# Loading and turning the second half's input in counted steps of the v block and the next, a longer end of the mLSTM, and written order up to the last projection block

## The chip, the core and the metric

The kernel runs on one core of a Trainium2 chip. The metric is device time in microseconds (us) for one execution. PE is the matrix engine; its weight loads have a row of their own, PEld. DVE is the vector engine, ACT the scalar engine and POOL the GpSimd engine. SP issues the DMAs. Each engine carries out its own instructions strictly in the order in which the program lists them, and waits on semaphores for the others.

## What is computed

One layer of a hybrid decoder trunk on 2048 positions of 1024 channels, in fp32. Cut to what matters here:

```python
h = rms_norm(x, g_mix) * (1 + sc1) + sh1
p = h @ w_in            # q_a k_a v_a | q_m k_m v_m o_m | u_s v_s | gates
y_attn  = forgetting_attention(rms(q_a), rms(k_a), v_a, f_a)   # 8 heads of 64
y_mlstm = sigmoid(o_m) * rms(mlstm_chunkwise(q_m, k_m, v_m, i_m, f_m))
y_sgu   = spatial_gating(gelu(u_s), gelu(v_s))
x = x + gt1 * (concat(y_attn, y_mlstm, y_sgu) @ w_out)
x = x + gt2 * conv_ffn(rms_norm(x, g_ffn) * (1 + sc2) + sh2)
```

The change touches the first part alone: the norm of x, the projections p, and the mLSTM that runs beside them.

## The kernel before

**Products.** Every fp32 operand is split into a high and a low part, and a product is three matmuls (`mm3`, lines 54 to 56: high by high, high by low, low by high). The sequence is cut into two halves of 1024 positions, and each half into 8 row tiles of 128. `hT[tb, k]` holds h turned (channels on the partitions) for one block `tb` of 512 positions and one of 8 channel groups `k`, as a high tile `hh` and a low tile `hl`.

**Blocks.** The projection runs as 14 steps, n = 0 to 13: seven blocks of columns of `w_in` for the first half (n = 0 to 6), then the same seven for the second (n = 7 to 13). The order of the seven is km with the gates (272 columns), qm and om (512), vm (256), the spatial gating's u and v (512), attention k (512), attention q (512), attention v (512). A block has eight row tiles; one row tile is 8 x 3 matmuls into a PSUM tile `acc`. There are three such tiles until the last block and two in it (`n_accs`). After a row tile a consumer reads it. In the v block this is `use_v` (line 754): twice per row tile, ACT casts 256 columns to the high part (line 761), DVE subtracts for the low part (line 762), and SP stores the pair to `v_d` (line 763). The pair is a tile `vhl` of the tag `q2k`, which has three buffers, shared with `qn` of the q block.

**Ticks.** `tick` (line 627) is the hook through which other work is laid between the matmuls. It runs at the end of each row tile and, in a block of 512 columns, also in its middle (after k = 3), so a wide block has 16 ticks and a narrow one 8. A tick runs what is due (`after(n, f)` puts a function n ticks ahead, such as the turning of q), one step of `rest_of_mod` in a middle tick (one DMA of a 256 KB piece `wa` of `w_ada`, one DVE operation on the piece before), and one step of the first generator in the list `background`: `rows`, `mlstm`, and in the last block `scores`. A generator gives the turn back at each `yield`. `products` (line 599) also loads (`load`) and casts (`cast`) the weights of the next block: one load at the end of each of the row tiles 0 to 6 and one in tile 7, the casts from tile 4 on, four of them in tile 7 and the last behind the block.

**The mLSTM's end.** `mlstm(qi)` handles 512 positions in 21 ticks. In its last five (lines 1027 to 1055) DVE divides H, ACT squares it into `hq` (line 1038), DVE reduces (line 1040), POOL raises to the power -0.5 (line 1042), two ticks on DVE multiplies into `hq` (line 1045), and two further ticks on PE turns `hq` (line 1052).

**The second half's input.** At step 6 four tiles of x are asked for (`load_x`, line 402). At step 7, ahead of the km block's matmuls, `make_h(2, x0)` and `make_h(3)` (line 555) norm and turn the half's two blocks: per row tile two squares on ACT (line 518), the mean and power, a multiplication on DVE (line 523); per channel group four transposes on PE (line 560), an ACT activation (line 564) and a DVE cast and subtraction (lines 565, 566).

**Who sets the order.** Steps 1 to 5 and 8 to 12 stand in a `manual_schedule`: there the order on each engine is that of the program's text. Steps 0, 6, 7 and 13 are ordered by a scheduler, which may draw an instruction forward past others, also into a written stretch. Step 13 closes the pools of the projection's side, opens attention's, loads k, the forget bias `nf`, q and the first half of v of head 0 (`load_k`, `load_q`, `load_v`), and puts the scores of head 0's first two blocks into `background`, from its first tick on.

Of the kernel before, what the change touches and what calls it, by code (L numbers as in the profile page):

```python
# [17 lines left out]
P = 128  # L18
S = 2048
D = 1024  # L20
DFF = 2816
NH = 8
EPS = 1e-6
NEG = -1.0e30
TB = 512
KT = D // P
# [7 lines left out]
def trunk(  # L34
# [43 lines left out]
    ident = cst.tile([P, P], F32, name="ident")  # L78
# [11 lines left out]
    a1 = cst.tile([P, KT], F32, name="a1")  # L90
    sh1 = cst.tile([P, KT], F32, name="sh1")
# [280 lines left out]
    def tr_ps():  # L372
        return pp.tile([P, 512], F32, name="trp", tag="trp")

    def misc_ps():
        return pp.tile([P, 512], F32, name="mp", tag="mp")
# [25 lines left out]
    def load_x(tt):  # L402
        xt = pool.tile([P, D], F32, name="xt", tag="t4k")
        dma(xt, x[tt * P : (tt + 1) * P, :])
        return xt
# [17 lines left out]
    def rest_of_columns():  # L423
        r = pool.tile([P, P], F32, name="rows", tag="tmpA")
        dma(r[0:8], g_ffn[0].rearrange("(k p) -> k p", p=P))
        for i, g in enumerate((g_q, g_k)):
            for j in range(2):
                dma(r[8 + i : 9 + i, 64 * j : 64 * j + 64], g)
        dma(r[10:14], b_s[0])
        dma(r[14:16], g_m_out[0].rearrange("(k p) -> k p", p=P))  # L430
        transposed(colA[:, 24:40], r, 16)
        V.tensor_scalar(gq8, colA[:, 32:33], 0.125, None, op0=ALU.mult)
# [80 lines left out]
    def norm_x(xin):  # L513
        for xt in xin:
            st = pool.tile([P, 2], F32, name="st", tag="st")
            for q in range(2):
                jk = pool.tile([P, 512], F32, name="jk", tag="sq")
                A.activation(jk, xt[:, q * 512 : q * 512 + 512], AF.Square, accum_out=st[:, q : q + 1])
            V.tensor_tensor(st[:, 0:1], st[:, 0:1], st[:, 1:2], op=ALU.add)
            st = st[:, 0:1]  # L520
            V.tensor_scalar(st, st, 1.0 / D, EPS, op0=ALU.mult, op1=ALU.add)
            rsqrt(st, 1)
            V.tensor_scalar(xt, xt, st, None, op0=ALU.mult)
        return xin

    x0 = norm_x([load_x(i) for i in range(4)])
# [7 lines left out]
    def head_setup():  # L534
        rest_of_columns()
        dma(gsgu, g_sgu.broadcast_to([P, 256]))
        dma(gbias[:, 0:8], b_fox_f.broadcast_to([P, 8]))
        dma(gbias[:, 8:12], b_m_i.broadcast_to([P, 4]))
        dma(gbias[:, 12:16], b_m_f.broadcast_to([P, 4]))
        wsn = pool.tile([P, 4, P], F32, name="wsn", tag="sq")  # L540
        dma(wsn, w_s[0].rearrange("g t s -> t g s"))
        for g in range(4):
            G.affine_select(
                wsn[:, g, :], wsn[:, g, :], pattern=[[-1, P]], compare_op=ALU.is_ge, fill=0.0,
                base=0, channel_multiplier=1,
            )
        ps = misc_ps()
        for g in range(4):
            T.transpose(ps[:, g * P : (g + 1) * P], wsn[:, g, :], ident)
        A.copy(wT.rearrange("p g t -> p (g t)"), ps)  # L550


    hT = {}

    def make_h(tb, xin=None):
        xs = xin if tb == 0 else norm_x(xin or [load_x(tb * 4 + i) for i in range(4)])
        for k in range(KT):
            ps = (tr_ps, acc_ps)[k % 2]() if tb == 0 else tr_ps()
            for i in range(4):
                T.transpose(ps[:, i * P : (i + 1) * P], xs[i][:, k * P : (k + 1) * P], ident)  # L560
            h32 = pool.tile([P, TB], F32, name="h32", tag="t2k")
            hh = pool.tile([P, TB], F32R, name="hh", tag="hT")
            hl = pool.tile([P, TB], F32R, name="hl", tag="hT")
            A.activation(h32, ps, AF.Identity, bias=sh1[:, k : k + 1], scale=a1[:, k : k + 1])
            V.tensor_copy(hh, h32)
            V.tensor_tensor(hl, h32, hh.bitcast(F32), op=ALU.subtract)  # L566
            hT[tb, k] = (hh, hl)


    class Weights:  # L570
# [51 lines left out]
    pending = []  # L622
    chores, started = [], []
    background = []
    ticks = [0]

    def tick(middle=False):
        ticks[0] += 1
        due()
        if middle and chores and started and next(chores[0], True):  # L630
            chores.pop(0)
        if background and next(background[0], True):
            background.pop(0)
# [19 lines left out]
    def due(everything=False):  # L653
        for item in pending[:]:
            if everything or item[0] <= ticks[0]:
                pending.remove(item)
                item[1]()
# [267 lines left out]
    def mlstm(qi):  # L925
        t0 = qi * 512
        neb = nebs[qi % 2]
        ecol, acol, dcol = cols[qi]
        H = pool.tile([P, 4, 4, 65], F32, name="H", tag="H")
# [48 lines left out]
        for n in range(4):  # L978
            kT, M1 = got["k", n], got["M", n]
            kn, qT, v1 = got["l", n]  # L980
            qz = qzs[n % 2]
            sc = pool.tile([P, 4, P], F32, name="sc", tag="sc")
# [53 lines left out]
        dma(om, om_d[:, :, t0 : t0 + 512].rearrange("j p t -> p j t"))  # L1036
        hq = pool.tile([P, 4, 4, 64], F32, name="hq", tag="t4k")
        A.activation(hq, hn, AF.Square)
        ss = pool.tile([P, 4, 4], F32, name="mss", tag="mss")
        V.tensor_reduce(ss, hq, axis=AX.X, op=ALU.add)  # L1040
        V.tensor_scalar(ss, ss, 1.0 / 64, EPS, op0=ALU.mult, op1=ALU.add)
        G.tensor_tensor(ss, ss, nhalf[:, 0:1].unsqueeze(2).broadcast_to([P, 4, 4]), op=ALU.pow)
        yield
        yield
        V.tensor_tensor(hq, hn, bc(ss, 3, 64), op=ALU.mult)
# [21 lines left out]
    nb = len(blocks)  # L1067
    steps = [(h, i) for h in range(2) for i in range(nb)]
    chores.append(rest_of_mod())
    written = ExitStack()  # L1070
# [4 lines left out]
        cur.cast()  # L1075
    first_mod(1)
    for n, (half, i) in enumerate(steps):
        if i == 0:
            make_h(half * 2, x0)
            if half == 0:  # L1080
                head_setup()
            make_h(half * 2 + 1)
        elif n == nb - 1:
            x0 = [load_x(8 + t) for t in range(4)]
        if n == len(steps) - 1:
            while background:
                if next(background[0], True):
                    background.pop(0)
            n_accs[0] = 2
            pool.close("proj_r")  # L1090
            pp.close("proj_r")
            attention_open_right()

            load_k(0)
            first_rows = [], []
            first = [scores(0, tb, load_q(0, tb, "qA"), r) for tb, r in zip((1, 0), first_rows)]
            load_v(0, (0, 1))
            background += first
        nxt[0] = Weights(blocks[steps[n + 1][1]][0]) if n + 1 < len(steps) else None
        if i == 1:  # L1100
            written.enter_context(tc.manual_schedule())
        blocks[i][1](half, cur)
        started.append(n)
        if nxt[0]:
            nxt[0].cast()
        cur = nxt[0]
        if n in (nb - 2, 2 * nb - 2):
            written.close()
        if i == 0:
            log_gates(half)  # L1110
            background += [rows(half * 2), rows(half * 2 + 1)]
        if i == 2:
            background.append(mlstm(half * 2 + 1))
        if n == nb + 2:
            small_setup()
    while pending:
        due(True)
    pool.close("proj_l")
    pp.close("proj_l")

# [37 lines left out]
    hT = {}  # L1158
# [33 lines left out]
    class Block:  # L1192
# [466 lines left out]
    for i, s in enumerate(steps):  # L1659
# [33 lines left out]
        if i:  # L1693
            q = steps[i - 1]
# [51 lines left out]
```

## Time and profile before

| | us |
|---|---|
| median of 3 runs | 2610.47 |
| lowest and highest | 2605.68, 2610.91 |
| the profiled execution | 2607.8 |
| its span on the core | 2606.1 |

The profiled execution lies 2.7 below the median of the three. The span is the stretch from the first instruction to the last, and 1.7 lies around it. The page of the profile gives each engine's busy time; a PE that is busy isn't a PE at its peak, because overlapping matmuls are counted as busy at any pitch. The view of waits lists, for one engine, the idle time before its instructions and what ended it. The timeline lists instructions in order of time: start, duration, engine, line, operation, what is written and read, and in square brackets the idle time of the engine before it. The view of windows gives busy time for each engine in a stretch, the granted PE clock (PEclk), and the DMA engines' share and rate. The projection fills the first 711 us of the span; the rest is attention, the output projection and the channel MLP.

### The profile page before, as it was taken

To read this page: it belongs to the slowest core of one execution; us is meant where nothing else is said; L and a number is where in the kernel's file an instruction comes from. 1 tells how busy PE (TensorE), PEld (TensorE's weight loads), DVE (VectorE), ACT (ScalarE), POOL (GpSimd) and SP (SyncE) were. 2 spreads that over 40 slices of the span, in tenths; PEclk is the share of its full clock that TensorE was granted. 3 is DMA by queue.
4 is the path that set the end of the run, shared out by engine and by line. 5 is a ranking of instruction groups with operands and counts; after the bars stand their busy time and mean duration, and the time that the engine had idled before them with its cause. 6 is when DMAs were issued, how large, how long until landed. Compare 5 with 4: busy or idle time off the path is not lost.

```text
span 2606.1 us, 36311 instructions
## 1 busy us (share of the span) xinstructions
PE 2530.5 (97%) x12521; PEld 2097.9 (81%) x12537; DVE 2010.0 (77%) x3438; ACT 1272.8 (49%) x2424; POOL 402.5 (15%) x532
## 2 busy tenths in 40 slices
PE   5999999999999999999989999999999999999999
PEld 5888888888787877777868888888888888888787
DVE  7657666476388889866589888888888887997797
ACT  4333343432388878844455544454444444444443
POOL 2012310132266556520000000000000000000000
PEclk9999999999999999999999999999999999999999
DMA  7345763454664445266632222255222217658523
GB/s 247 107 120 160 209 209 88 129 152 138 180 164 123 129 126 166 58 195 224 248 89 92 79 89 82 81 201 187 90 81 81 90 65 279 210 176 290 184 93 117
DMA packets 302592, 379.58 MB, mean 146 GB/s; under 512 B 31934, under 2 KB 194588, under 8 KB 300360
## 3 DMA queue, kind: packets, MB, share of 16 engines
q1 hardware_dynamic: 302408, 377.26, 46.1%
q8 instruction: 99, 1.62, 0.3%
q14 instruction: 85, 0.70, 0.1%
HBM read 276.44 MB, written 100.74 MB: 145 GB/s over the span
## 4 chain that ended last, share of the span: by engine, by line
PE 81%; DVE 9%; DMA 4%; ACT 3%; issue 2%; POOL 1%; SPq 0%; DVEq 0%; ACTq 0%; POOLq 0%
PE ub L56 11%; PE ub L54 11%; PE ub L55 11%; PE acc L54 6%; PE acc L56 6%; PE acc L55 6%; PE db L55 4%; PE db L56 4%; PE db L54 4%; PE sp L206 3%; PE tp L259 3%; PE op L245 2%; PE op L246 2%; PE wps L55 2%; PE wps L54 2%
## 5 line engine op out<-in xcount | busy, mean ns | idle before, releaser
L54 PE MATMUL acc<-wh,hh 128*128 128x512 f32 (+2 forms) x768 | 285.5, 373 | 1.9 <-DVE vhl L762 1.2
L54 PE MATMUL ub<-T,wsph 128*128 128x512 f32 x704 | 274.2, 390 | 5.8 <-ACT wsph L1358 5.8
L56 PE MATMUL ub<-T,wspl 128*128 128x512 f32 x704 | 273.7, 389 | 1.6 <-DVE wspl L1359 1.6
L56 PE MATMUL acc<-wh,hl 128*128 128x512 f32 (+2 forms) x768 | 274.2, 360 | 0.3 <-DVE hl L566 0.3
L55 PE MATMUL acc<-wl,hh 128*128 128x512 f32 (+2 forms) x768 | 273.9, 358 | 0.2
L55 PE MATMUL ub<-T,wsph 128*128 128x512 f32 x704 | 273.9, 389 | 0.0
L55 PE MATMUL db<-wspl,wsph 128*128 128x512 f32 x616 | 240.6, 391 | 3.6 <-DVE wspl L1490 3.5
L56 PE MATMUL db<-wsph,wspl 128*128 128x512 f32 x616 | 239.6, 389 | 0.0
L54 PE MATMUL db<-wsph 128*128 128x512 f32 x616 | 238.3, 389 | 0.3 <-ACT wsph L1489 0.3
L1358 ACT CAST wsph<-S 128x512 fp32r<-128x512 f32 x176 | 109.7, 623 | 228.4 <-PE ub L55 162.8
L263 DVE TENSOR_TENSOR plo<-tp,phi 128x512 fp32r<-128x512 f32 (+1 forms) x320 | 187.0, 607 | 31.6 <-ACT phi L262 29.4
L54 PE MATMUL ub<-B,wsph 128*128 128x512 f32 x528 | 207.1, 392 | 2.8 <-ACT wsph L1358 2.8
L56 PE MATMUL ub<-B,wspl 128*128 128x512 f32 x528 | 207.2, 392 | 0.6 <-DVE wspl L1359 0.6
L55 PE MATMUL ub<-B,wsph 128*128 128x512 f32 x528 | 207.0, 392 | 0.0
L223 ACT ACTIVATE L<-L,nm 128x1024 f32<-128x1024 f32 (+2 forms) x192 | 172.6, 903 | 36.0 <-DVE nm L212 34.7
L262 ACT CAST phi<-tp 128x512 fp32r<-128x512 f32 (+1 forms) x320 | 160.0, 521 | 40.2 <-PE tp L259 38.9
L259 PE MATMUL tp<-ident,L 128*128 128x128 f32 x1088 | 177.0, 274 | 2.5 <-POOL L L228 0.6
L206 PE MATMUL sp<-kk,q 128*128 128x512 f32 (+3 forms) x640 | 169.2, 375 | 3.3 <-DVE nm L212 2.2
L1489 ACT CAST wsph<-act 128x512 fp32r<-128x512 f32 x132 | 82.3, 623 | 179.0 <-PE db L55 162.2
L228 POOL TENSOR_SCALAR L<-L,rs 128x1024 f32<-128x1024 f32 (+2 forms) x192 | 167.2, 881 | 11.0
L56 PEld LDWEIGHTS acc<-wh,hl 128*128 128x128 f32 x768 | 145.0, 190 | 22.3 <-DVE hl L566 0.8
L54 PEld LDWEIGHTS acc<-wh,hh 128*128 128x128 f32 x768 | 146.2, 191 | 20.7 <-DVE vhl L762 1.4
(333 smaller groups left out, 5942.9 us busy)
## 6 DMA issues: line engine op xcount, KB each, us to landing
w<-in_w_up_dram SPq DMA_DIRECT2D x88, 512.0 KB
wd<-in_w_down_dram SPq DMA_DIRECT2D x176, 256.0 KB
wa<-in_w_ada_dram SPq DMA_DIRECT2D x96, 256.0 KB
act_d<-yc SPq DMA_DIRECT2D x44, 512.0 KB
act<-act_d SPq DMA_DIRECT2D x44, 512.0 KB
wr<-in_w_in_dram SPq DMA_DIRECT2D x64, 256.0 KB
q<-q_d SPq DMA_DIRECT2D x128, 128.0 KB
hc_d<-hl SPq DMA_DIRECT2D x28, 512.0 KB
```

Source lines behind the costliest of these rows:

```text
L54: T.matmul(ps, lh, rh, start=start, stop=False, skip_group_check=resume)
L55: T.matmul(ps, lh, rl, start=False, stop=False, skip_group_check=resume)
L56: T.matmul(ps, ll, rh, start=False, stop=stop, skip_group_check=resume)
L206: T.matmul(sp[:, b : b + bw], q2[n][:, qs], kk[:, s0 + b : s0 + b + bw], start=n == 0, stop=n == 1 and not last)
L223: A.activation(L[c], L[c], AF.Exp, bias=nm[:, n - 1 : n], scale=-1.0, accum_out=rs[:, c : c + 1])
L228: G.tensor_scalar(t, t, rs[:, 0:1], 1.0, op0=ALU.mult, op1=ALU.mult)
L245: T.matmul(op[:, c0:], vv[:, j, :], hi[:, c0:], start=(j == 0), stop=False)
L259: T.transpose(tp[:, i * P : (i + 1) * P], rows[i][j // 8][:, (j % 8) * P : (j % 8 + 1) * P], ident)
L262: A.copy(hi[:, c0:], tp[:, c0:])
L263: V.tensor_tensor(lo[:, c0:], tp[:, c0:], hi[:, c0:].bitcast(F32), op=ALU.subtract)
L1358: A.copy(hi, src)
L1489: A.copy(hi, v)
```

## The change

Five things are done.

- **Input of block 2.** At the start of step 6 `ahead(2, ...)` issues the four loads of x, and lays the rest into the plan: squares of row tile i at tick 2 + i of step 6, mean and power one tick on, scaling two ticks on, and one `turn_h` (4 transposes, activation, cast, subtraction) at each of the ticks 8 to 15.
- **Input of block 3.** At the same place `ahead(3, ...)` issues its four loads, into a fifth `t4k` buffer, into the mLSTM's tile `H`, and as two pieces each into the `M1` and the `sc` buffers. Squares start at tick 8 of step 6; the turns lie two by two at the ticks 0 to 3 of step 7.
- **mLSTM.** Its end gets a `yield` between square and reduction and one more behind the power: 23 ticks.
- **Scores.** The scores in step 13 start five ticks later.
- **Order.** One `manual_schedule` holds from step 1 to the end of step 13.

```diff
+    def ahead(tb, n, t0, places, turns):
+        xs, sts = [], []
+        for i, tag in enumerate(places):
+            src = x[(tb * 4 + i) * P : (tb * 4 + i + 1) * P, :]
+            if tag in ("t4k", "H"):
+                t = pool.tile([P, D], F32, name="xt", tag=tag)
+                dma(t, src)
+                xs.append([t[:, 0:512], t[:, 512:1024]])
+            else:
+                xs.append([pool.tile([P, 512], F32, name="xp", tag=tag) for _ in range(2)])
+                for q in range(2):
+                    dma(xs[i][q], src[:, q * 512 : q * 512 + 512])
...
+        def scale(i):
+            for q in range(2):
+                V.tensor_scalar(xs[i][q], xs[i][q], sts[i][:, 0:1], None, op0=ALU.mult)
+        for i in range(4):
+            for d, f in enumerate((squares, stats, scale)):
+                at(n, t0 + i + d, lambda f=f, i=i: f(i))
+        for k, (nk, t) in enumerate(turns):
+            at(nk, t, lambda k=k: turn_h(tb, k, lambda i: xs[i][k // 4][:, k % 4 * P : k % 4 * P + P], tr_ps()))
...
     def tick(middle=False):
         ticks[0] += 1
+        for f in plan.pop((started[-1] + 1 if started else 0, block_tick[0]), ()):
+            f()
+        block_tick[0] += 1
         due()
...
         A.activation(hq, hn, AF.Square)
+        yield
         ss = pool.tile([P, 4, 4], F32, name="mss", tag="mss")
...
         G.tensor_tensor(ss, ss, nhalf[:, 0:1].unsqueeze(2).broadcast_to([P, 4, 4]), op=ALU.pow)
+        yield
         yield
         yield
...
         elif n == nb - 1:
-            x0 = [load_x(8 + t) for t in range(4)]
+            assert not background
+            ahead(2, n, 2, ("t4k",) * 4, [(n, 8 + k) for k in range(KT)])
+            ahead(3, n, 8, ("t4k", "H", "M1", "sc"), [(n + 1, k // 2) for k in range(KT)])
...
-            background += first
+            background += [(None for _ in range(5)), *first]
...
-        if n in (nb - 2, 2 * nb - 2):
-            written.close()
...
     while pending:
         due(True)
+    assert not plan
+    written.close()
```

More of the change, by code (lines that the diff above doesn't have):

```diff
@@ L555, in make_h @@
     def make_h(tb, xin=None):
-        xs = xin if tb == 0 else norm_x(xin or [load_x(tb * 4 + i) for i in range(4)])
+        xs = xin if tb == 0 else norm_x([load_x(tb * 4 + i) for i in range(4)])
         for k in range(KT):
[L558 to L567, printed above, removed]
+            turn_h(tb, k, lambda i: xs[i][:, k * P : (k + 1) * P], (tr_ps, acc_ps)[k % 2]() if tb == 0 else tr_ps())
@@ new lines, in ahead, with squares, stats @@
+    def ahead(tb, n, t0, places, turns):
[10 more added lines that the diff above has]
+                    dma(xs[i][q], src[:, q * 512 : q * 512 + 512])
+        def squares(i):
+            st = pool.tile([P, 2], F32, name="st", tag="st")
+            for q in range(2):
+                jk = pool.tile([P, 512], F32, name="jk", tag="sq")
+                A.activation(jk, xs[i][q], AF.Square, accum_out=st[:, q : q + 1])
+            sts.append(st)
+        def stats(i):
+            st = sts[i]
+            V.tensor_tensor(st[:, 0:1], st[:, 0:1], st[:, 1:2], op=ALU.add)
+            V.tensor_scalar(st[:, 0:1], st[:, 0:1], 1.0 / D, EPS, op0=ALU.mult, op1=ALU.add)
+            rsqrt(st[:, 0:1], 1)
+        def scale(i):
+            for q in range(2):
+                V.tensor_scalar(xs[i][q], xs[i][q], sts[i][:, 0:1], None, op0=ALU.mult)
[4 more added lines that the diff above has]
+            at(nk, t, lambda k=k: turn_h(tb, k, lambda i: xs[i][k // 4][:, k % 4 * P : k % 4 * P + P], tr_ps()))
@@ new lines, in trunk, with at, turn_h @@
+    plan = {}
+    def at(n, t, f):
+        plan.setdefault((n, t), []).append(f)
+    def turn_h(tb, k, piece, ps):
+        for i in range(4):
+            T.transpose(ps[:, i * P : (i + 1) * P], piece(i), ident)
+        h32 = pool.tile([P, TB], F32, name="h32", tag="t2k")
+        hh = pool.tile([P, TB], F32R, name="hh", tag="hT")
+        hl = pool.tile([P, TB], F32R, name="hl", tag="hT")
+        A.activation(h32, ps, AF.Identity, bias=sh1[:, k : k + 1], scale=a1[:, k : k + 1])
+        V.tensor_copy(hh, h32)
+        V.tensor_tensor(hl, h32, hh.bitcast(F32), op=ALU.subtract)
+        hT[tb, k] = (hh, hl)
@@ L624, in trunk @@
     background = []
-    ticks = [0]
+    ticks, block_tick = [0], [0]
     def tick(middle=False):
         ticks[0] += 1
+        for f in plan.pop((started[-1] + 1 if started else 0, block_tick[0]), ()):
+            f()
+        block_tick[0] += 1
         due()
@@ L1077, in trunk @@
     for n, (half, i) in enumerate(steps):
[L1078 to L1082, printed above, removed]
+        block_tick[0] = 0
+        if n == 0:
+            make_h(0, x0)
+            head_setup()
+            make_h(1)
         elif n == nb - 1:
-            x0 = [load_x(8 + t) for t in range(4)]
+            assert not background
+            ahead(2, n, 2, ("t4k",) * 4, [(n, 8 + k) for k in range(KT)])
+            ahead(3, n, 8, ("t4k", "H", "M1", "sc"), [(n + 1, k // 2) for k in range(KT)])
         if n == len(steps) - 1:
-            while background:
-                if next(background[0], True):
-                    background.pop(0)
+            assert not background
             n_accs[0] = 2
@@ L1097, in trunk @@
             load_v(0, (0, 1))
-            background += first
+            background += [(None for _ in range(5)), *first]
         nxt[0] = Weights(blocks[steps[n + 1][1]][0]) if n + 1 < len(steps) else None
-        if i == 1:
+        if n == 1:
             written.enter_context(tc.manual_schedule())
```

## The prediction

> **What bounds the kernel now.** The page first, for the span; then PE's waits inside the projection, 60 to 730 us, the only part that the change touches.
>
> ```profile
> span 2606.1 us, 36311 instructions
> PE mps L1052 <- DVE hq L1045: 6.8, 4, 2.7
> PE trp L560 <- ACT h L564: 2.1, 1, 2.1
> PE acc L54 <- DVE vhl L762: 1.2, 1, 1.2
> ```
>
> The columns of a wait are its total, how often, and the longest. PE waits in three places only: four times for `hq` at the mLSTM's end (6.8), around step 7's transposes, and in step 13 for the release of an `acc`. Each of the change's edits aims at one of them. PE sets the end elsewhere, so what is taken out of or put into PE's stream in the projection should reach the end one to one. I cost the three places in turn.
>
> **Input of the second half.** The stretch from the end of step 6's matmuls to the first of step 8, as a window; the pitch of the km block's matmuls in the timeline; four transposes in the chain of waits; then the other engines' part of a turn.
>
> ```profile
> 372.20:408.80 36.60, 33.51 (x258) 31.68 (x257) 25.42 (x59) 22.38 (x45) 1.65 (x3) 1.00 0.43 143
> 380.13 0.29 PE L54 MATMUL acc<-wh,hh 128*128 128x272 f32 x1
> 380.25 0.29 PE L55 MATMUL acc<-wl,hh 128*128 128x272 f32 x1
> 332.39 0.44 PE trp L784 x4
> L564 ACT ACTIVATE h<-trp,sh,a x16: 767/777/804, 374.5 to 397.0; 128x512 f32<-128x512 f32 x16
> L565 DVE CAST hh<-h x16: 417/420/428, 375.3 to 399.6; 128x512 fp32r<-128x512 f32 x16
> L566 DVE TENSOR_TENSOR hl<-h,hh x15: 683/691/693, 375.8 to 399.0; 128x512 fp32r<-128x512 f32 x15
> L523 DVE TENSOR_SCALAR xt<-xt,st x16: 746/753/756, 8.0 to 390.2; 128x1024 f32<-128x1024 f32 x16
> L596 DVE TENSOR_TENSOR wl<-wr,wh 128x272 fp32r<-128x272 f32 x8 | 3.4, 439 | 0.7 <-ACT wh L595 0.7
> L468 DVE SCALAR_TENSOR_TENSOR modacc<-wa,cs,modacc 128x512 f32<-128x512 f32 x13 | 9.7, 746 | 5.0 <-DMA wa<-in_w_ada_dram 5.0
> L762 DVE TENSOR_TENSOR vhl<-acc,vhl x32: 404/425/427, 336.7 to 712.0; 128x256 fp32r<-128x256 f32 x32
> ```
>
> PE has 192 matmuls there at a pitch of 0.125 (24.0) and 16 turns at 0.44 (7.0): 31.0 of work in 36.6. So 5.6 is the most that can be won, though the busy column shows only 3.1 idle; the rest is loose pitch. The transposes move, they don't vanish.
>
> What remains behind the change, at two joints. At the end of step 6 the last turn (ACT 0.78, DVE 0.42 + 0.69), two `vhl` subtractions (0.42 each) and the cast of the last weight (0.44) are in line on DVE: 0.44 + 0.78 + 1.11 + 0.84 + 0.44 = 3.6 behind the row tile, while PE asks for that weight after 0.44 + 7 x 3 x 0.125 + 0.13 = 3.2. With lags between engines I take 0.9 (0.4 to 1.5). At tick 3 of step 7 two turns come just ahead of the tile that needs them: the last low part is ready after 0.44 + 2 x 0.78 + 2 x 0.69 = 3.4, asked for after 0.88 + 21 x 0.125 + 0.25 = 3.8; I take 0.5 for lag (0 to 1). In ticks 10 to 13 of step 6 DVE has, per row tile, two turns (2.2), two scalings (1.5), two `vhl` (0.84), a weight cast (0.44) and a w_ada piece (0.75) = 5.7, under PE's 5.44 + 0.88 = 6.3: covered, with little to spare. The squares are as many as before and now run on ACT behind the matmuls.
>
> The loads are the risk: ten DMAs, 4.2 MB, are now issued at once at the start of step 6, and SP, ACT and DVE all stand behind them. The comparable burst is step 13's, which exists before too: SP's and ACT's timeline, and windows.
>
> ```profile
> 659.63 1.20 SPq L157 DMA_DIRECT2D kk<-k_d  x2
> 672.60 2.00 SPq L763 DMA_DIRECT2D v_d<-vhl  x2
> 663.21 0.37 ACT L761 CAST vhl<-acc 128x256 fp32r<-128x256 f32 x1 [3.80 <-PE acc L56]
> 694.42 0.37 ACT L761 CAST vhl<-acc 128x256 fp32r<-128x256 f32 x1 [4.21 <-PE acc L56]
> 699.86 0.37 ACT L761 CAST vhl<-acc 128x256 fp32r<-128x256 f32 x1 [4.21 <-PE acc L56]
> 660.00:665.00 5.00, 5.00 (x25) 4.14 (x25) 2.35 (x4) 1.32 (x3) 1.95 (x1) 1.00 1.02 245
> 665.00:670.00 5.00, 5.00 (x25) 4.14 (x25) 0.45 (x2) 0.38 (x1) 0.00 (x0) 1.00 0.98 308
> 670.00:675.00 5.00, 5.00 (x25) 4.09 (x23) 0.42 (x1) 0.57 (x2) 0.00 (x0) 1.00 1.10 255
> 675.00:680.00 5.00, 4.18 (x25) 3.07 (x23) 4.14 (x11) 3.19 (x7) 2.60 (x4) 1.00 0.82 263
> 680.00:685.00 5.00, 3.61 (x17) 2.55 (x18) 3.52 (x12) 4.22 (x13) 4.80 (x9) 1.00 0.64 191
> L404 SPq DMA_DIRECT2D xt<-in_x_dram x16: 343/424/580, 1.3 to 380.8; - x16
> L518 ACT ACTIVATE jk<-xt x32: 612/622/642, 5.2 to 387.5; 128x512 f32<-128x512 f32 x32
> 3.50:9.00 5.50, 0.18 (x1) 0.18 (x2) 1.97 (x12) 3.77 (x11) 1.12 (x3) 1.00 1.01 395
> ```
>
> Two casts 5.44 apart give a row tile of a wide block. The first load of the burst is issued 3.6 before tile 0's cast, and the first `v_d` store only 13 us after that load, since it is queued behind the loads. `vhl` has three buffers, two of them held by `qn` when the block begins: the second `vhl` of tile 1 needs the buffer of that first store. Until the store has landed, ACT stands at this cast and tile 1's `acc` is not free.
>
> In step 6 tile 0 ends at 332.4 (the chain row above), so the loads go out at 328.8. Up to and with the first store SP has 4.2 (x) + 0.26 + 0.14 (w_ada, km weights) + 0.52 (q) + 0.26 = 5.4 MB. Loads of x ran at 395 GB/s at the kernel's start, the last window; the mean of the four windows from 660 to 680 is 268. The kernel's first x (asked for at 1.3, squared from 5.2) took 3.9, 1.3 of it its 0.52 MB, so 2.6 passes ahead of the first data. The store lands at 328.8 + 2.6 + 13.7 = 345.1, or + 20.1 = 351.5. Cast and subtraction, 0.9, later `acc` is free: 346.0 or 352.4. With three `acc` PE needs it at tile 4, 332.4 + 3 x 5.44 + 2 x 0.44 = 349.6: no wait, or 2.8. Behind that ACT cast stand the squares of tiles 2 and 3, then on DVE and POOL statistics, power and scaling, about 6 us; the first turn at tick 8 wants them at 352.3: no wait, or 3.2. Most of the bytes are x in long rows, so I take the fast end: nothing. Sum: -5.6 + 1.4 = **-4.2** (-5.6 to +1.8).
>
> **The mLSTM's end.** The timeline of DVE and POOL at the first of the four waits, and PE's wait at the third.
>
> ```profile
> 206.29 1.22 DVE L1040 TENSOR_REDUCE mss<-hq 128x16 f32<-128x1024 f32 x1 [1.19 <-ACT hq L1038]
> 207.80 3.27 POOL L1042 TENSOR_TENSOR mss<-mss,nhalf 128x16 f32<-128x16 f32 x1 [3.88 <-DVE mss L1041]
> 211.04 0.91 POOL L712 TENSOR_TENSOR ev<-ev 128x256 f32<-128x256 f32 x1
> 211.98 0.42 DVE L716 TENSOR_REDUCE mu<-ev 128x4 f32<-128x256 f32 x1 [0.51 <-POOL ev L712]
> 213.17 1.22 DVE L1045 TENSOR_TENSOR hq<-H,mss 128x1024 f32<-128x1024 f32 x1
> 214.31 0.68 DVE L596 TENSOR_TENSOR wl<-wr,wh 128x512 fp32r<-128x512 f32 x1
> 214.53 1.06 PE L1052 MATMUL mps<-ident,hq 128*128 128x128 f32 x8 [2.69 <-DVE hq L1045]
> 216.24 0.69 DVE L596 TENSOR_TENSOR wl<-wr,wh 128x512 fp32r<-128x512 f32 x1
> 545.89 1.06 PE L1052 MATMUL mps<-ident,hq 128*128 128x128 f32 x8 [2.69 <-DVE hq L1045]
> ```
>
> Two waits of 2.69 lie at the end of the spatial-gating block (steps 3 to 4, 10 to 11); the two others sum to 6.8 - 5.4 = 1.4 and lie in quiet ticks: these go (-1.4). The 2.69 I don't believe gone. PE stands ready at 211.84 after k = 3 of step 4's first tile; DVE, 5 us behind, still has that step's last two weight casts to do, which PE meets at k = 6 and 7. Without the stop PE asks for the first low part at 211.7 + 2 x 0.68 + 0.23 = 213.3. DVE: `hq` (1.14) leaves the line, but the reduction now runs a tick on, behind a weight cast and a gating step, from about 207.8 to 209.0; the power after it ends at 212.2, and only then comes POOL's 0.91 for the gating's variance, for which DVE waits until 213.15 instead of 211.98. So DVE starts that cast at 214.3, as before, and ends it at 215.0: PE waits 1.7. The last cast slips by 0.4, to 217.3, and PE asks at 215.7: 1.6 more. That is 3.3 in place of 2.69 with, at the same point, the transposes still to be paid; net +0.4 each (all gone, -2.7; or +1.0 where the power runs late). Two of them: +0.9. Sum: **-0.5** (-6.8 to +0.6).
>
> **Step 13.** In the windows above PE is idle 0.82 + 1.39 = 2.2 from 675 to 685, and the scores fill the rest of that hole: the scheduler put them where tile 3's `acc` was still held. In written order they come at tick 6, the middle of tile 3, behind the very wait. Bytes up to the first store: 3.1 for k, nf and q, 0.52 for v, 0.52 for q's stores, 0.26 = 4.4 MB; the first three windows moved 1.23 + 1.54 + 1.28 = 4.05 of it by 675, the rest needs 1.5 at 263 GB/s. Landing 676.5 at the least; with the store's completion I take 678 (to 680), `acc` free at 678.9. With two `acc` PE needs it at tile 3: 663.2 + 2 x (0.44 + 5.44) = 675.0. So 3.9 (2.4 to 5.9) goes in, 2.2 comes out: **+1.7** (-2.2, if the scores' hole closes and no wait comes, to +3.7).
>
> The Trainium skill (DMA: Bandwidth & Descriptors, Anatomy of one DMA) gives every DMA about 2.0 us beside its bytes; by that the store lands at 678.5 and the sum grows by 0.5. It speaks against the change only in size.
>
> **Sum.** -4.2 - 0.5 + 1.7 = -3.0. The profiled execution took 2607.8, so 2604.8. It lies 2.7 under the median of the three runs; the range takes that in. The longer written stretch by itself I cost at nothing: steps 1 to 5 and 8 to 12 are written already, and PE's only waits in them are the mLSTM's.
>
> **The rivals.**
> *All three holes close* (the weight casts come in time, the store doesn't hold the last block): -6.8 - 5.6 - 2.2 = -14.6, 2593; partly so, up to 2600. For it: the waits are real idle time of PE, and 36.6 against 31.0 is counted work. Against it: the casts' times above.
> *Slower: stores queued behind loads.* One mechanism in both v blocks: ACT, at the `vhl` cast, waits for a store that SP put behind 4 MB. It decides when step 6's first store lands later than 348.7, 19.9 after the loads begin. At 268 GB/s step 6 loses 6.0, at the late end step 13 loses 3.7, each wait halves PE's clock once after it (1.7, next rival): -4.2 + 6.0 - 0.5 + 3.7 + 3.4 = +8.4, 2616. For it: step 13's store was issued 13 us after its loads. Against it: x moves at 395.
> *The clock falls after step 13's wait.*
>
> ```profile
> 1227.00:1230.68 3.68, 1.55 (x15) 1.31 (x12) 1.91 (x4) 0.96 (x2) 0.00 (x0) 1.00 0.51 136
> 1230.68:1234.10 3.42, 3.03 (x12) 2.66 (x13) 3.31 (x6) 3.42 (x6) 0.00 (x0) 0.50 0.76 212
> 214.80:218.20 3.40, 3.40 (x21) 2.90 (x20) 2.79 (x9) 0.00 (x0) 0.97 (x2) 1.00 0.16 58
> ```
>
> After 1.55 busy in 3.68 the clock stood at 0.50 for 3.42; after the 2.69 at 211.84 it stayed at 1.00. With 3.9 idle in place of 2.69 a half-speed stretch would cost half of 3.42: +1.7, 2606.5. The Trainium skill (TensorE: Matmul & The Clock Gate, Part 1) says that an idle window of about 3.4 us halves the clock, the windows running free; both rows agree with it, and by it the wait of 3.9 may or may not fill a window.
>
> **How the numbers follow.** Forecast 0.45 (its own range 2600 to 2611), all holes close 0.25, slower 0.17, clock 0.13. The range 2596 to 2616 leaves out the better half of the second and little of the third. A measurement of this kernel tells 0.2% (5.2) from no change. Faster: 0.25 and a fifth of 0.45, 0.34; slower: 0.15 of the third and 0.02 of the others, 0.17; the same: 0.49.
>
> **What would show it.** Step 7's stretch near 32.5 between the first km matmul and step 8, with no wait on `xt`; in step 4's first tile a PE wait for `wl` (line 596) of some 3 us and none at line 1052; in step 13 a PE wait for `vhl` of some 4 us ahead of tile 3, the scores behind it. I am wrong if tile 3 starts without a wait, if PE waits at tile 4 or at the first turn of step 6, or if `wl` holds PE for less than 1.5.

## The result and the profile after

| | before | after |
|---|---|---|
| median of 8 runs each | 2606.20 us | 2615.62 us |
| lowest and highest | 2603.15, 2610.91 | 2612.14, 2618.44 |
| ratio, 95% interval | | 1.0032 [1.0021, 1.0043] |
| span of the profiled execution | 2606.1 us | 2616.4 us |

The changed kernel is slower by 9.4 us. The forecast was 2605, no change that can be told. (Of the experiments below, one of the eleven executions of e3, 6560.81 us, and one of the eleven of e6, 8951.57 us, were far slower than all others and are left out of the ratios.) The page's first line and PE's waits of the changed kernel, in the stretch of the projection (total, how often, the longest):

```profile
span 2616.4 us, 36335 instructions
PE acc L55 <- DVE wl L640: 5.3, 4, 1.4
PE acc L54 <- DVE vhl L809: 4.2, 1, 4.2
PE trp L604 <- DVE xt L589: 2.6, 2, 1.9
PE mps L1050 <- DVE sc L1036: 1.5, 2, 0.7
PE acc L54 <- ACT wh L639: 0.9, 1, 0.9
PE mps L1101 <- DVE hq L1094: 0.6, 1, 0.6
```

The 6.8 of waits for `hq` are gone but for 0.6. In their place PE waits for the weights' low part (`wl`), the wait for `vhl` has grown from 1.2 to 4.2, and the second half's turns (now line 604) wait for `xt`. To see what this costs, the windows are cut at the first matmul of a step: 4 and 5, 6 and 7, 11 and 12, and 13. The columns are length, then busy time of PE, PEld, DVE, ACT, POOL, the granted PE clock, DMA share and rate. First before, then after.

```profile
208.83:326.50 117.67, 114.04 (x595) 95.59 (x598) 79.43 (x163) 36.52 (x74) 37.68 (x25) 1.00 0.67 196
326.50:408.65 82.15, 79.06 (x467) 69.23 (x466) 50.27 (x116) 39.66 (x92) 7.22 (x9) 1.00 0.55 174
540.18:657.44 117.26, 114.02 (x584) 94.55 (x586) 76.14 (x155) 37.45 (x76) 37.68 (x25) 1.00 0.56 160
657.44:710.51 53.07, 50.86 (x236) 41.23 (x235) 15.84 (x38) 14.35 (x35) 12.05 (x17) 1.00 0.62 184
```

```profile
209.41:329.51 120.10, 116.13 (x599) 96.72 (x598) 78.15 (x162) 35.67 (x73) 36.72 (x25) 0.99 0.58 165
329.51:413.10 83.59, 79.88 (x467) 69.65 (x466) 52.29 (x124) 38.63 (x92) 9.17 (x10) 0.98 0.63 204
544.66:665.11 120.45, 117.07 (x587) 96.61 (x586) 76.34 (x157) 37.44 (x76) 37.97 (x25) 0.97 0.54 155
665.11:722.25 57.14, 52.90 (x236) 42.61 (x235) 16.18 (x38) 14.61 (x35) 11.96 (x17) 0.94 0.57 171
```

All four stretches are longer: by 2.43, 1.44, 3.19 and 4.07, together 11.1 of the 11.7 by which the projection ends later (722.25 instead of 710.51). Idle time explains 3.1 of it, 2.0 of that in step 13; the other 8.0 is PE's busy time. In steps 11 and 12 PE's busy column grew by 3.05 with the same work, and the last column but two says why: the clock was 1.00 everywhere before and is 0.97 there now, 0.94 in step 13. A mean of 0.97 over 120.45 is about 7 us at half speed. So the question for the experiments was double: which wait replaced which, and what the clock made of it.

### The profile page after: what moved, and what is told of

Its sections match the earlier page's. It is cut to its first block, busy times and chain, and to the rows that moved or that the text cites. A ratio compares the mean times of both kernels' runs of the same rounds, so it can differ in the third digit from the quotient of the medians.

```text
span 2616.4 us, 36335 instructions
## 1 busy us (share of the span) xinstructions
PE 2538.9 (97%) x12537; PEld 2104.6 (80%) x12537; DVE 2013.1 (77%) x3446; ACT 1271.8 (49%) x2424; POOL 402.4 (15%) x532
## 4 chain that ended last, share of the span: by engine, by line
PE 76%; DVE 10%; DMA 6%; issue 3%; ACT 3%; POOL 2%; SPq 1%; DVEq 0%; ACTq 0%; POOLq 0%
PE ub L56 11%; PE ub L54 10%; PE ub L55 10%; PE acc L55 5%; PE acc L54 5%; PE acc L56 5%; PE db L55 4%; PE db L56 4%; PE db L54 4%; PE sp L206 4%; PE tp L259 3%; PE op L245 2%; PE op L246 2%; PE wps L55 2%; PE wps L56 2%
## 5 line engine op out<-in xcount | busy, mean ns | idle before, releaser
L55 PEld LDWEIGHTS acc<-wl,hh 128*128 128x128 f32 x768 | 148.2, 193 | 26.7 <-DVE wl L640 8.3
```

What stands on the lines that cost most here:

```text
L55: T.matmul(ps, lh, rl, start=False, stop=False, skip_group_check=resume)
```

## The experiments

Each ran beside the kernel before on its own chip: e1 to e7 on one, e8 and e9 on another. So the ratios compare kernels better than the medians do. Stage lengths are the same four windows, in each kernel's profiled execution, which is one of the 8 to 12 behind its median; "half" is the time at a granted clock of 0.50 inside the projection. At half speed at most half of a stretch can be lost.

| kernel | median | ratio to before | 4+5 | 6+7 | 11+12 | 13 | half |
|---|---|---|---|---|---|---|---|
| before | 2606.2 to 2609.1 | | 117.67 | 82.15 | 117.26 | 53.07 | 0 |
| after | 2615.62 | 1.0032 [1.0021, 1.0043] | 120.10 | 83.59 | 120.45 | 57.14 | 20.5 |
| e1 short end | 2609.93 | 1.0007 [0.9999, 1.0016] | 117.70 | 79.56 | 118.77 | 56.83 | 17.1 |
| e2 filled wait | 2616.39 | 1.0031 [1.0020, 1.0042] | 118.53 | 83.72 | 120.59 | 55.84 | 10.2 |
| e3 later q and v | 2608.54 | 1.0004 [0.9995, 1.0013] | 119.87 | 83.96 | 117.72 | 50.96 | 13.7 |
| e4 later x | 2612.10 | 1.0018 [1.0009, 1.0028] | 118.53 | 80.52 | 117.98 | 55.87 | 3.4 |
| e5 end behind the joint | 2609.41 | 1.0001 [0.9992, 1.0009] | 120.06 | 79.53 | 116.88 | 56.16 | 6.8 |
| e6 three edits | 2605.55 | 0.9982 [0.9974, 0.9991] | 119.80 | 80.35 | 116.87 | 50.34 | 3.4 |
| e7 before + two steps | 2616.90 | 1.0030 [1.0021, 1.0040] | 118.59 | 86.24 | 119.21 | 54.49 | 10.2 |
| e8 short end, later q and v | 2603.86 | 0.9980 [0.9971, 0.9989] | 117.71 | 79.53 | 118.88 | 51.24 | 10.2 |
| e9 second step only | 2608.80 | 1.0002 [0.9993, 1.0012] | 120.52 | 79.63 | 119.52 | 50.61 | 10.2 |

(In e1, e3 and e8, 6.8 of the half-speed time is in step 0, which has its own waits for the first loads.)

### e1: the mLSTM's end as long as before

```diff
         A.activation(hq, hn, AF.Square)
-        yield
...
         G.tensor_tensor(ss, ss, nhalf[:, 0:1].unsqueeze(2).broadcast_to([P, 4, 4]), op=ALU.pow)
-        yield
         yield
         yield
```

> The changed kernel with the mLSTM's end as long as before (both added steps removed), all else as changed. My theory (the wait for hq was only turned into two waits for the weight's low part, and these, split and with little work between them, put PE's clock to half for 3.41 and 6.83 us): the stops at hq return, 2.69 at steps 4 and 11, PE's waits for wl go, no half-speed stretch in steps 4, 11 and 12. Steps 4+5 fall from 120.11 to about 117.9, steps 11+12 from 120.45 to about 117.5, about 5 in all: 2610 to 2611, ratio to the kernel before about 1.0015. Rival (the waits alone cost, the clock is beside the point): PE's waits for hq are 6.8 in all where those for wl and hq were 5.9, so the time stays or rises by 1: about 2616.

Measured 2609.93: 5.7 under the changed kernel by the medians, 6.5 by the ratios, about as the theory had it. Steps 4 and 5 are back at 117.70. Steps 11 and 12 took 118.77 and not 117.5: a half-speed window stands behind the wait for `hq` there, which the theory had excluded. And the largest gain is where the theory had not looked, in steps 6 and 7: 83.59 to 79.56. A half window less explains under half of it (1.7); the rest is the waits. The timeline of SP, DVE, ACT and PE in step 6, first of the changed kernel, whose step 6 begins at 329.51, then of e1, whose step begins at 325.52:

```profile
331.40 0.38 SPq L838 DMA_DIRECT2D q_d<-qhi  x1
332.66 0.75 DVE L836 SCALAR_TENSOR_TENSOR qlo<-trp,gq,qhi 128x512 fp32r<-128x512 f32 x1
333.43 0.38 SPq L838 DMA_DIRECT2D q_d<-qlo  x1
333.86 3.31 SPq L567 DMA_DIRECT2D xt<-in_x_dram  x6
346.16 1.02 SPq L810 DMA_DIRECT2D v_d<-vhl  x2
351.63 0.37 ACT L808 CAST vhl<-acc 128x256 fp32r<-128x256 f32 x1 [7.80 <-DMA v_d<-vhl]
359.67 0.33 PE L604 MATMUL trp<-ident,xt 128*128 128x128 f32 x1 [1.91 <-DVE xt L589]
```

```profile
326.52 0.75 DVE L836 SCALAR_TENSOR_TENSOR qlo<-trp,gq,qhi 128x512 fp32r<-128x512 f32 x1 [0.30 <-ACT qhi L835]
327.30 0.38 SPq L838 DMA_DIRECT2D q_d<-qlo  x1
327.73 3.29 SPq L567 DMA_DIRECT2D xt<-in_x_dram  x6
339.90 1.21 SPq L810 DMA_DIRECT2D v_d<-vhl  x2
353.23 0.33 PE L604 MATMUL trp<-ident,xt 128*128 128x128 f32 x1 [0.71 <-DVE xt L589]
```

SP issues in order, so the loads of x stand behind a store of the q block, and that store waits for DVE's `qlo`. With the long end it goes out 3.92 after the step's start, with the short one 1.78. Each 512-position chunk of the mLSTM now takes two ticks more, so the second chunk ends four ticks later: its `hq` is turned 34.5 into step 5 (at 310.9), and 21.2 into it in the kernel before (at 296.0). DVE enters step 6 2.1 later (3.92 less 1.78). The loads are late by as much, the first `v_d` store with them (ACT stands 7.80 at the cast that needs its buffer), then the squares, then the turns.

### e7: the two steps alone, on the kernel before

```diff
+        yield
...
+        yield
```

(at the same two places of the kernel before)

> The kernel before with nothing but the two steps added to the mLSTM's end. Theory (at the joints the wait for hq turns into two for wl and one for sc, 0.7 longer in sum, and where a window of the clock falls on them PE runs at half for 3.41 or 6.83 us): steps 4+5 118.5 to 120.1 and 11+12 117.8 to 120.5 instead of 117.67 and 117.26, with 3 to 6 on the time: 2611 to 2614, ratio 1.001 to 1.0022. Rival (the longer end costs only in company with the new input of the second half): no change, 2608.

Measured 2616.90, a ratio of 1.0030: more than the theory's upper end, and as much as the whole change. Its windows say where: 4+5 and 11+12 as forecast (+0.9, +2.0), +1.4 in step 13 behind a half-speed window, and again steps 6 and 7, 86.24 instead of 82.15, here with the kernel's old input. PE's timeline shows a wait there, in step 6's first row tile, that the kernel before does not have:

```profile
334.22 0.79 PE L55 MATMUL acc<-wl,hh 128*128 128x512 f32 x1 [2.51 <-DVE wl L596]
```

The weight's low part comes late from DVE, as `qlo` did in the changed kernel. The two steps make DVE late at the start of step 6 whatever stands there. The rival, that they cost only in company, is out.

### e3: less ahead of the store in step 13

```diff
-            first = [scores(0, tb, load_q(0, tb, "qA"), r) for tb, r in zip((1, 0), first_rows)]
-            load_v(0, (0, 1))
+            q00 = []
+            first = [scores(0, 1, load_q(0, 1, "qA"), first_rows[0]), scores(0, 0, q00, first_rows[1])]
+            at(n, 4, lambda: q00.extend(load_q(0, 0, "qA")))
+            at(n, 8, lambda: load_v(0, (0, 1)))
```

> The changed kernel in whose step 13 the second q of the first head pair is loaded at tick 4 and its v at tick 8 instead of at the step's start: about 1 MB less lies ahead of the first v_d store on SP. Theory (the store behind the loads holds vhl, acc and so PE): at some 280 GB/s the store lands 3.7 earlier, the wait of 4.24 ahead of tile 3 falls under 0.6, no half-speed stretch, and step 13 falls from 57.13 to 50.5 to 51.5: about 6 faster, 2609 to 2610. Rival (the written order itself costs, or another holder of acc): the wait stays over 3 and step 13 over 55.

```profile
PE acc L54 <- DVE vhl L809: 0.4, 1, 0.4
660.73:711.69 50.96, 50.57 (x236) 40.92 (x235) 16.17 (x38) 14.59 (x35) 11.96 (x17) 1.00 0.63 192
```

As expected, in the wait, the stage and the time. The step is now 2.1 shorter than before the change: the hole that the scores used to fill is gone too. So written order by itself costs nothing that shows here; the bytes ahead of the store cost 6.2, of which the wait is 3.85 (4.24 less 0.39) and the rest, 2.3, is clock.

### e2: the wait in step 13 filled with work

```diff
+            def filler():
+                ps, hh = tr_ps(), hT[2, 0][0]
+                for _ in range(18):
+                    T.matmul(ps, hh[:, 0:P], hh, start=True, stop=True)
+            at(n, 5, filler)
```

> The changed kernel with 18 matmuls 512 wide, whose result nothing reads, put at tick 5 of step 13, ahead of the tile that waits for vhl; they are added work of about 4.1 us on PE at full speed, about as long as the wait, and free only what it lasts. Theory (clock): PE's wait shrinks from 4.24 to under 0.5, the half-speed stretches of 6.83 in step 13 go, and step 13 falls from 57.13 to about 54.5 although PE does 4 us more work: about 2.5 faster, ratio about 1.0025. Rival (the clock costs nothing there, the loss is the wait and the order): step 13 stays at 57.1 or rises by what the fill overlaps badly.

Windows of the changed kernel over the wait, then e2's wait and its step 13:

```profile
682.70:685.17 2.47, 0.00 (x0) 0.00 (x0) 0.72 (x2) 0.00 (x0) 0.00 (x0) 1.00 1.13 373
685.17:688.60 3.43, 1.66 (x4) 1.40 (x5) 1.21 (x4) 0.74 (x2) 0.00 (x0) 0.50 1.06 354
688.60:692.00 3.40, 3.40 (x9) 2.63 (x9) 0.42 (x1) 0.37 (x1) 0.00 (x0) 0.50 0.51 161
692.00:695.40 3.40, 3.40 (x18) 2.82 (x18) 0.83 (x2) 0.92 (x2) 0.52 (x1) 1.00 0.48 136
```

```profile
PE acc L54 <- DVE vhl L809: 1.2, 1, 1.2
662.34:718.18 55.84, 54.64 (x254) 44.29 (x253) 16.10 (x38) 14.59 (x35) 11.96 (x17) 1.00 0.58 175
```

In 3.40 at a clock of 0.50 the changed kernel starts 9 matmuls, in the next 3.40 at 1.00 it starts 18 (some small ones among them): half speed is real speed. With PE kept busy in the wait no window is at half, and step 13 is 1.3 shorter, not the 2.5 that was expected: 1.2 of wait stayed behind the fill. From the lengths, 57.14 less 3.0 of wait and plus 4.1 of fill (the estimate written down before) would be 58.2; 55.84 came, and the 2.4 between agrees with e3's 2.3. The median of the whole run did not fall (2616.39), so this part is shown in the stage only.

### e4: the second block's loads of x at tick 4

```diff
-            ahead(3, n, 8, ("t4k", "H", "M1", "sc"), [(n + 1, k // 2) for k in range(KT)])
+            at(n, 4, lambda n=n: ahead(3, n, 8, ("t4k", "H", "M1", "sc"), [(n + 1, k // 2) for k in range(KT)]))
```

> The changed kernel in whose step 6 the loads of the second half's second block of x go out at tick 4 instead of at the step's start, behind the first v_d store. Theory (the store behind the loads, then ACT's squares behind the cast, then the turn): the store lands some 5 us earlier, PE's waits for xt (2.6) go, the half-speed stretch of 3.41 at 360.9 goes, and steps 6+7 fall from 83.58 to 79 to 80: about 4 faster, ratio about 1.002. Rival (the turns inside the v block cost what they do wherever their input comes from): steps 6+7 stay over 82.5. A third outcome: the loads come late for the squares at ticks 8 to 11, and PE waits at the second block's first turn in step 7.

```profile
PE trp L604 <- DVE xt L589: 1.3, 1, 1.3
325.87:406.39 80.52, 78.20 (x468) 68.69 (x466) 52.27 (x124) 38.71 (x92) 8.71 (x10) 1.00 0.66 212
```

3.1 off steps 6 and 7, no half speed there, and 3.5 off the median (3.7 by the ratios). The wait for `xt` is halved, not gone. So the bytes ahead of the store matter, and with e1 there are two ways to the same 3 to 4 us: fewer bytes, or the loads on time.

### e5: the end moved behind the joint

```diff
+        if qi % 2 == 0:
+            for _ in range(5):
+                yield
         den = pool.tile([P, 4, 4], F32, name="den", tag="den")
```

(with the short end)

> The changed kernel with the mLSTM's end as long as before, but for the chunks whose end would fall at the joint of the gating block and the next (every second one) it begins five ticks later, so that it lies inside steps 4 and 11 and not across their start. Theory (at that joint DVE and POOL have gating, weight casts and the mLSTM's scale at once, and whatever comes last there holds PE; a few ticks on it is quiet): no wait for hq of 2.69 and none for wl, steps 4+5 about 115.0 and 11+12 about 114.6 (before 117.67 and 117.26), about 5.5 under the run with the end as long as before: 2604, ratio 0.9985. Rival (the end costs its wait wherever it falls, since its power and scale are late by construction): PE waits for hq over 2 in ticks 2 to 6 of steps 4 and 11, and the time is that of the run with the short end, 2610.

```profile
311.38 1.42 PE L1103 MATMUL mps<-ident,hq 128*128 128x128 f32 x8 [2.86 <-DVE hq L1096]
208.78:328.84 120.06, 116.03 (x596) 96.66 (x598) 78.70 (x161) 35.92 (x72) 36.66 (x24) 0.99 0.58 169
```

A miss: 2609.41 instead of 2604, and 120.06 in steps 4 and 5 instead of 115.0. The wait at the joint of steps 3 and 4 went, and one of 2.86 came up inside step 5, where the second chunk's end had been pushed, with a half-speed window behind it. Steps 11 and 12 gained 1.9 against e1, most of it a half window that e1 had there. The rival was nearer in the time (2610). The waits that it looked for in ticks 2 to 6 did not come; one of the same size came in the next step.

### e9: one of the two added steps

e8's kernel with the step between power and scale kept.

> The run with the short end and q and v of step 13 at ticks 4 and 8, but with one of the two added steps kept, the one between the mLSTM's power and its scale. Theory (what makes the weight's casts late is the first added step, which moves the reduction and the power behind gating, so that POOL's product for the gating waits for the power; the second alone takes the scale out of DVE's line): power over by 211.0 to 211.5 of a first gating block as before, no wait for hq of 2.69, PE's waits for wl at the joint under 1.2 in all instead of 2.6, steps 4+5 115.5 to 117 and 11+12 115 to 116.5; 2 to 4 under the run with the short end: about 2600 to 2601, ratio 0.997. Rival (each added step costs, whichever it is, since DVE stands a tile later at the next joints): waits for wl over 2 or a wait for xt over 2 in step 6, and 2605 or more.

DVE and PE at the first joint (timeline):

```profile
214.49 0.50 PE L55 MATMUL acc<-wl,hh 128*128 128x512 f32 x1 [0.50 <-DVE wl L640]
215.07 1.22 DVE L1093 TENSOR_TENSOR hq<-H,mss 128x1024 f32<-128x1024 f32 x1
217.20 0.69 DVE L640 TENSOR_TENSOR wl<-wr,wh 128x512 fp32r<-128x512 f32 x1
217.94 0.80 PE L55 MATMUL acc<-wl,hh 128*128 128x512 f32 x1 [2.49 <-DVE wl L640]
```

The first weight cast is in time, as the theory had it (a wait of 0.50), but the scale now stands ahead of the last cast, and PE waits 2.49 for that. 0.50 + 2.49 is 2.99, where the changed kernel has 1.27 + 1.36 = 2.63 and the kernel before 2.69. Three orders of the same DVE work, three times about the same wait: DVE is behind at this joint, and the order only chooses for what PE waits. The second chunk's end comes two ticks later instead of four (28.1 into step 5), and step 6 isn't late: steps 6 and 7 take 79.63, so that half of the rival falls. The other half came: a wait for `wl` over 2, and a time of 2608.80 instead of 2600 to 2601, 4.9 above e8 beside the same runs of the kernel before.

### e6 and e8: the parts together

> The changed kernel with three edits together: the mLSTM's end short and five ticks later at the joints, the second block's loads of x at tick 4 of step 6, and q and v of step 13 at ticks 4 and 8. Theory (the parts are independent, each wait's price its own length and the half-speed stretches it makes): from 2615.6 -5.7 for the short end, -5.5 for its place, -3.5 for the loads of x, -7 for step 13: about 2594, ratio about 0.9945; no half-speed stretch between 60 and 720 us. Rival (waits move on: what is taken out at one joint comes in at the next): above 2600.

> The changed kernel with the mLSTM's end as long as before and q and v of step 13 at ticks 4 and 8; the loads of x stay at the start of step 6. Theory now (the two added steps also made DVE, and by it SP's loads of x, late into step 6; with them away the later loads of x are not needed, and the end is best where it was): steps 6+7 about 79.6 (80.35 with the loads at tick 4), 4+5 about 117.7, step 13 about 50.5 to 51; in all 5.5 to 6 under the run with the short end alone, 2603 to 2604, ratio 0.998, no worse than the three edits together. Rival (the loads of x need their place behind the first store): steps 6+7 over 80.5, and slower than the three edits together.

e6 (e3, e4 and e5 in one) takes 2605.55, far from the 2594 that adding the parts gave: e5's part gives nothing that can be told, and e4's part gives nothing once the end is short, since both mend the same store. With e8 (e1 and e3 alone) steps 6 and 7 take 79.53 instead of e6's 80.35, and the time is 2603.86, a ratio of 0.9980 [0.9971, 0.9989]: no worse than e6's, faster than the kernel before by 4.3 on the same chip, and faster than the changed one, which stands at 1.0032. What e8 keeps of the change is the new input, the written order and the scores' later start.

## Why the prediction went wrong

**The step that failed** is the price of the mLSTM's longer end. It was worked out at the two joints alone; the two other ends were written off as "quiet ticks: these go", and the loads of x were taken at their old place in SP's queue. What came instead: these ends come four ticks later, the one in step 5 makes DVE, and by it SP's loads of x, 2.1 late into step 6, and steps 6 and 7 lost 1.4 where 4.2 were to be won. The second step that failed is the clock, which the sum put at nothing; it cost about 2 at the joints, 2.3 in step 13, and up to 1.7 behind the late turn in step 6.

**Input of the second half: the mechanism right, one term wrong.** The store behind the loads, ACT at the cast, the squares and the late first turn were all named, with "no wait, or 3.2"; the fast end was taken, and PE waited 2.6 at the first turn, one of the prediction's own signs of being wrong. With the short end (e1) it was the right end: the loads go out 2.2 after the step's start (the prediction's 328.8 was 2.3), PE waits 0.71, and steps 6 and 7 win 2.6. Of the 4.2 expected the rest is pitch: PE's idle time went from 3.09 to 1.73, but its busy time fell only by 1.2. The term that failed is the issue time of the loads: it was taken from the trace of before, as if the mLSTM's longer end left SP's queue where it was. It came 4.35 after the step's start, and +1.4 stands where -4.2 was forecast. The marker for step 7 (32.5) was ill placed: half of the turns lie in step 6 now, step 7 takes 29.3 (383.79 to 413.10), and only 6 and 7 together tell. The wait at step 7's first row tile, foreseen at 0.9 for DVE's low part, came as 0.9 for ACT's high part (`wh`).

**The mLSTM's end: the joint right, the rest wrong.** At the joints the wait for `wl` was foreseen at 3.3 and is 2.63. (3.3 in place of 2.69 would be +0.6 each; the prediction wrote +0.4 and gives no reason.) The two other ends do not vanish; the one in step 5 comes four ticks later and leaves DVE late for step 6, which is worth 4.0 (e1's 79.56 against 83.59). A wait of 0.7 for `sc` inside each of steps 4 and 11 was not seen. The term was -0.5. Undoing the two steps gives 5.7, and making them alone costs 7.8 on the kernel before.

**Step 13: right in size without the clock.** A wait of 3.9 in, 2.2 out was the forecast; 4.24 came in, and e3 shows 2.1 out. The step lost 4.07 and not 1.7, and what is missing is about e3's remainder, 2.3: the clock. The section of the Trainium skill that the prediction names for its 2.0 us (DMA: Bandwidth & Descriptors, Anatomy of one DMA) tells of DMAs that GpSimd issues. Here SP issues them, and the step's first `v_d` store took 4.85 from issue to landing (680.75 to 685.61).

**The clock was put down as a rival with one window.** The prediction gave it 1.7, behind step 13 alone, and let the waits at the joints pass, since one of 2.69 had left the clock at 1.00. It quoted the rule that the windows run free, and did not carry it to the joints. And its own row, 1.55 busy of 3.68 ahead of a stretch at 0.50, did not agree with an idle window, as it said: PE was not idle there. These windows, 3.41 long and cut on the grid on which each trace's clock changes, show the same joint with the same instructions in two executions, first the changed kernel's, then e2's:

```profile
214.13:217.54 3.41, 0.96 (x3) 0.48 (x3) 3.04 (x7) 0.62 (x1) 1.79 (x2) 1.00 0.98 338
217.54:220.95 3.41, 3.35 (x8) 2.68 (x9) 2.84 (x5) 0.60 (x1) 1.91 (x2) 0.50 0.17 67
```

```profile
211.39:214.80 3.41, 2.15 (x9) 1.12 (x7) 2.58 (x6) 0.62 (x1) 1.91 (x2) 1.00 1.01 320
214.81:218.22 3.41, 2.08 (x9) 1.75 (x10) 2.77 (x8) 0.60 (x1) 1.83 (x2) 1.00 0.60 203
218.22:221.63 3.41, 3.41 (x25) 3.10 (x24) 2.66 (x6) 0.00 (x0) 1.21 (x2) 1.00 0.00 0
```

Where both waits fall into one window, PE is busy for 0.96 of 3.41 and the next window runs at half. Where the border lies between them, both windows are over 2, and nothing happens. It is chance where the border lies: of the four kernels whose steps 4 and 5 have the same text (after, e2, e3, e4) two show it there (120.10, 119.87) and two don't (118.53, 118.53), and in steps 11 and 12 again two (120.45, 120.59) and two not (117.72, 117.98). So the one wait of 2.69 that had passed without harm was luck, not a rule: in e8 the wait for `hq`, 2.7 at both joints, cost nothing at step 4, and at step 11 it left PE 0.71 of a window (steps 11 and 12 took 118.88):

```profile
540.42:543.83 3.41, 0.71 (x5) 0.31 (x4) 2.87 (x6) 1.91 (x5) 2.09 (x2) 1.00 0.82 243
543.83:547.24 3.41, 3.41 (x13) 3.02 (x13) 2.80 (x9) 0.00 (x0) 0.90 (x1) 0.50 0.40 143
```

**The sum.** Over those four traces steps 4 and 5 average 119.26 (+1.6 on before) and 11 and 12 average 119.19 (+1.9); with +1.4 in steps 6 and 7 and +4.1 in step 13 that is 9.0, and the medians differ by 9.4. Where no half-speed window falls, the two pairs of steps give +0.9 and +0.6; the other 2.1 of their 3.5 is the clock. Against the forecast's -3.0 that is 12.0: 5.6 missed in steps 6 and 7, 4.0 at the mLSTM's end, 2.4 in step 13. The rival "stores queued behind loads" gave 2616, by its own mechanism in steps 6 and 13, one halving behind each. It named both places, but that its number fits is partly luck: it makes +3.5 in steps 6 and 7 where +1.4 came, +5.4 in step 13 where +4.1 came, and -0.5 at the mLSTM's end where +3.5 came. Nor was its point of decision reached: the first store landed at 351.56, 17.7 after the loads began and not over 19.9. What made the turn late was above all that the loads began late: in e1 the store lands 16.9 after them (344.59), and PE waits 0.71.

## What to carry to other kernels

When a background job is made longer, follow its last piece to where it lands now, and see what stands behind the engine it lands on: here two ticks per chunk made DVE 2 us late a block further on, and SP, issuing in order, passed that on to ten loads and a store. An order that only chooses between equal waits on one busy engine gains nothing; fewer bytes ahead of a needed store do. And price a wait as its length plus, by chance, half of one or two clock windows, once it can leave PE busy for under 2.2 of one window of 3.41: here two waits of 2.63 together cost 1.3 to 2.7 more in four cases of eight, and nothing more in the other four.

## What the runs showed of the hardware

The clock's windows run on their own grid: in each of the eleven traces all stretches at 0.50 begin at whole multiples of 3.413 from each other, however the waits lie. The Trainium skill (TensorE: Matmul & The Clock Gate, Part 1) says that the windows run free and that an idle one of about 3.4 us throttles; the traces agree with both the length and the free run, but the window need not be idle. Between 60 and 2550 us of the eleven traces every full-speed window with PE busy for under 1.4 of 3.41 was followed by one at half, none with more than 2.21 was, and those between went both ways.

SP did not issue behind the burst as fast as it could. Three rows of its waits in the changed kernel from 337 to 347, in the same form as PE's:

```profile
SPq L629 <- DMA xt<-in_x_dram: 1.8, 2, 0.9
SPq L458 <- DMA xt<-in_x_dram: 1.0, 1, 1.0
SPq L810 <- DMA xp<-in_x_dram: 0.4, 2, 0.2
```

The issue of a weight load and of the `v_d` store waited for earlier loads of x to land. In the semaphore events of the same trace the ninth load of the burst is issued at 338.50, when the first has landed at 338.48; the tenth at 339.75, the second having landed at 339.74; the DMA behind them at 341.05, the third at 341.04. So in this stretch SP has eight DMAs under way at most, on eight semaphores that go round, and a long burst holds back the issue of what comes after it, not only its bytes: the first `v_d` store was issued 12.3 after the first load. The prediction counted the bytes alone.
